# A three-stage transformer kernel on one core: both token tiles share the first weight units, a broadcast by TensorE, one sine, decay rows by way of memory, an alternating solve, other buffers

## The chip, the core and the metric

The kernel runs on one core of a Trainium2 chip. A core has five engines with a queue each: TensorE (PE; its weight loads are PEld), VectorE (DVE), ScalarE (ACT), GpSimd (POOL) and SyncE (SP, which here issues most DMAs). The metric is the device time of one execution in microseconds.

## The reference

All arrays are float32, with 256 tokens of width 1024. A first block runs two layers, each of four sublayers with a norm before and after: a gated FFN (1024 to 2816 and back), a mixer, a cross attention to 256 memory rows, and a second gated FFN. A second block (a state-space branch and a windowed attention, then an FFN) follows.

```python
h = swiglu(rms_norm(x, norm_pre[l, 0]), ffn1_gate[l], ffn1_up[l], ffn1_down[l])
x = x + 0.5 * rms_norm(h, norm_post[l, 0])
h = parallel_head_groups(rms_norm(x, norm_pre[l, 1]), ...)      # the mixer
...
# in the mixer, four heads in two directions (forward and flipped), chunks of 64 tokens:
g = jnp.cumsum(g)                                               # log decays
decay = jnp.exp(jnp.where(tril, g[..., :, None] - g[..., None, :], -jnp.inf))
lower = jnp.where(strict, (k_beta @ k.T) * decay, 0.0)
sol = lax.linalg.triangular_solve(lower, rhs, lower=True, unit_diagonal=True)
```

## The kernel before

Tokens lie in two tiles of 128 (t = 0, 1). A float32 product is made of three passes over a high and a low part of each operand (`mm3`, L170 to L172). Weights arrive in units of 512 KB: SP loads a unit into one of four `raw` buffers (L143), ACT writes its high part (L148), DVE its low part (L149), in two halves each. The split units live in a pool: `wp` has 4 units, `w2`, open during the FFNs and the cross attention, has 8. A unit's buffer is free when its last product has read it.

The instruction order on each engine is not the program's. The library simulates the program when it is built: each engine takes the first instruction, in program order, whose inputs and buffers are ready in that simulation. `issue_after(ins)` and `fence` only add an order behind an instruction of the same engine. On the chip each engine then runs its queue strictly in that order.

**FFN.** The 2816 channels are eleven groups j. For j = 0 and 1 `by_tokens(t, j)` makes the products with the tokens as stationary side, 24 matmuls of 512 columns over four weight units, then tanh on ACT (L364) and two DVE steps (L365, L366); a tail (`flush`) transposes the result (L371). For j = 2 to 10 `by_channels(i, j)` uses 48 matmuls of 256 columns. `DN(t, j)` is the down projection, 12 matmuls of 512 columns over two units. Program order: by_tokens(0,0), by_tokens(0,1), DN(0,0), by_tokens(1,0), by_tokens(1,1), DN(0,1); for each j the two `by_channels`, with DN(0, j-1) and DN(1, j-1) between up to j = 7, and DN(0,7) at j = 8; then DN(0,8), (0,9), (0,10), `fin(0)`, DN(1,7), (1,8), (1,9), (1,10). `fin(t)` adds the residual and starts the next stage's norm: squares on ACT (L205), a reciprocal root by small steps on POOL, x (L300) and its product with the next gain, xg (L235, or L237 where the root is put in at once), on DVE. `take_pre(t)` transposes xg on PE (L250). `fin(1)` of a stage is kept in `late` and runs in the next one (`run_late`).

**Start.** 16 warm-up matmuls on zeros; SP issues x of tile 0, the first gain as a broadcast to 128 partitions (512 KB, L221), two weight units, x of tile 1, two units.

**Hooks.** The first FFN of a layer runs `setup` between its groups: rotary tables (a sine per token tile, L675, with an ACT table load), the mixer's parameters, the memory's norm.

**Mixer.** `fill` is a stream of projections, whose products keep PE busy; hooks between its quarters run the rest. `strengths` makes the log decays g; `decays(d)` lays out, for each direction, three sets of rows (cumulated g of a token tile, four heads, 128 columns, the same in all partitions) in PSUM: four matmuls against a triangle each (L805), and for two of them a matmul that adds a mask (L807). ACT takes the exponential into `E`, and `pairs` (DVE, L997) multiplies it in. `solve` works on the two directions' 64-row halves: steps of a product with `M` (L1145) or with an inverse (L1153), four heads for each direction.

## Time and profile before

| what | before |
|---|---|
| median of 3 runs | 1947.57 us (1945.8 to 1948.2) |
| the profiled execution's own time | 1947.42 us |
| its span, first to last instruction | 1945.2 us |
| PE busy | 1914.7 us (98%) |
| DVE, ACT, POOL busy | 73%, 54%, 10% |
| TensorE clock granted, mean | 0.998 |
| HBM read | 333.90 MB, 172 GB/s over the span |

The profile is of one execution. Busy time of PE is a union of modelled durations, so the distance between the starts of neighbouring matmuls says more than the busy share. "Idle before" a group is what its engine waited, with the releaser that ended most of it.

### The profile page before, as it was taken

The page shows a single profiled execution, that of the slowest core. Times are in us where ns is not written, and L with a number is a line of the kernel's source. Part 1 is how long each engine was busy: PE and PEld are TensorE (multiplying, and loading weights), DVE is VectorE, ACT ScalarE, POOL GpSimd, SP SyncE. Part 2 cuts the span into 40 slices and gives each one's busy share as a digit, 9 for nine tenths or more (in the row PEclk, how much of TensorE's full clock was granted, in tenths as well). Part 3 has the DMA queues.
Part 4 walks back from the last instruction along what each step waited for, and adds up shares of the span by engine and source line. Part 5 has one row for each costly group of instructions (what it writes and reads, how often), then busy time and mean ns, then how long its engine had stood idle before and what let it go on. Part 6 is the DMA issues. An engine that isn't in the chain of part 4 may idle for free.

```text
span 1945.2 us, 34675 instructions
## 1 busy us (share of the span) xinstructions
PE 1914.7 (98%) x12859; PEld 1717.7 (88%) x12859; DVE 1412.7 (73%) x3002; ACT 1048.9 (54%) x2173; POOL 185.7 (10%) x407
## 2 busy tenths in 40 slices
PE   9999999999999999999999999999999999999998
PEld 6899888898899989999788978998999998888997
DVE  6777688775666766667987757666798988767765
ACT  5655465465554555546555645554555555546542
POOL 2000100020200110010100120002101111001000
PEclk9999999999999999999999999999999999999999
DMA  8666434364566556644434726655566646656651
GB/s 266 206 220 217 125 109 147 109 220 137 164 205 196 180 186 220 187 161 144 137 101 145 247 86 212 200 189 157 146 174 182 187 121 205 200 196 224 199 179 49
DMA packets 272887, 337.26 MB, mean 173 GB/s; under 512 B 19740, under 2 KB 223150, under 8 KB 272718
## 3 DMA queue, kind: packets, MB, share of 16 engines
q1 hardware_dynamic: 266980, 326.64, 53.6%
q10 hardware_dynamic: 5690, 8.25, 1.2%
q8 instruction: 101, 1.65, 0.3%
q14 instruction: 68, 0.56, 0.1%
q0 software_dynamic: 48, 0.16, 0.0%
HBM read 333.90 MB, written 1.08 MB: 172 GB/s over the span
## 4 chain that ended last, share of the span: by engine, by line
PE 84%; DVE 4%; POOL 3%; DMA 2%; ACT 2%; issue 2%; SPq 0%; ACTq 0%; POOLq 0%; DVEq 0%
PE bank L170 25%; PE bank L171 25%; PE bank L172 25%; DVE lo L149 2%; DMA raw<-in_ffn_up_dram 2%; PE bank L250 1%; POOL t L192 1%; POOL vh L213 1%; POOL y L193 1%; ACT hi L148 1%; PE bank L1003 1%; PE bank L1543 1%; ACT md L1034 1%; PE bank L1153 1%; PE bank L1256 1%
## 5 line engine op out<-in xcount | busy, mean ns | idle before, releaser
L148 ACT ACTIVATE hi<-raw 128x512 fp32r<-128x512 f32 (+1 forms) x1190 | 678.7, 615 | 413.6 <-PE bank L172 96.0
L149 DVE TENSOR_TENSOR lo<-raw,hi 128x512 fp32r<-128x512 f32 (+1 forms) x1190 | 764.7, 680 | 187.1 <-ACT hi L148 178.4
L170 PE MATMUL bank<-xh,hi 128*128 128x256 f32 x2080 | 588.8, 283 | 0.0
L171 PE MATMUL bank<-xl,hi 128*128 128x256 f32 x2080 | 585.1, 281 | 0.0
L172 PE MATMUL bank<-xh,lo 128*128 128x256 f32 x2080 | 584.7, 281 | 0.1
L170 PEld LDWEIGHTS bank<-xh,hi 128*128 128x128 f32 x2080 | 394.2, 190 | 4.1
L171 PEld LDWEIGHTS bank<-xl,hi 128*128 128x128 f32 x2080 | 393.9, 189 | 3.5
L172 PEld LDWEIGHTS bank<-xh,lo 128*128 128x128 f32 x2080 | 394.5, 190 | 0.6 <-DVE lo L149 0.6
L170 PE MATMUL bank<-hi,xh 128*128 128x512 f32 (+1 forms) x852 | 333.5, 392 | 3.5 <-ACT xh L175 2.2
L171 PE MATMUL bank<-lo,xh 128*128 128x512 f32 (+1 forms) x852 | 324.7, 381 | 5.2 <-DVE lo L149 5.1
L172 PE MATMUL bank<-hi,xl 128*128 128x512 f32 (+1 forms) x852 | 323.9, 380 | 0.5 <-DVE xl L177 0.5
L171 PEld LDWEIGHTS bank<-lo,xh 128*128 128x128 f32 x852 | 160.3, 188 | 34.8 <-DVE lo L149 9.9
L170 PEld LDWEIGHTS bank<-hi,xh 128*128 128x128 f32 x852 | 160.2, 188 | 31.5 <-ACT xh L175 3.5
L172 PEld LDWEIGHTS bank<-hi,xl 128*128 128x128 f32 x852 | 159.9, 188 | 28.8 <-DVE xl L177 2.2
L170 PE MATMUL bank<-hi,hh 128*128 128x512 f32 x440 | 175.9, 400 | 1.3 <-ACT hh L175 1.3
L171 PE MATMUL bank<-lo,hh 128*128 128x512 f32 x440 | 173.9, 395 | 0.0
L172 PE MATMUL bank<-hi,hl 128*128 128x512 f32 x440 | 173.4, 394 | 0.0
L213 POOL TENSOR_SCALAR vh<-ss 128x1 f32<-128x1 f32 x40 | 27.6, 689 | 1130.8 <-ACT junk L205 996.1
L402 ACT ACTIVATE th<-s 128x256 f32<-128x256 f32 x90 | 37.3, 414 | 124.3 <-DVE s L401 122.7
L172 PEld LDWEIGHTS bank<-hi,hl 128*128 128x128 f32 x440 | 82.7, 188 | 20.7 <-DVE hl L177 0.3
L170 PEld LDWEIGHTS bank<-hi,hh 128*128 128x128 f32 x440 | 82.7, 188 | 18.4 <-ACT hh L175 1.7
L171 PEld LDWEIGHTS bank<-lo,hh 128*128 128x128 f32 x440 | 82.7, 188 | 16.0
(369 smaller groups left out, 1991.4 us busy)
## 6 DMA issues: line engine op xcount, KB each, us to landing
raw<-in_w_in_dram SPq DMA_DIRECT2D x112, 512.0 KB, 4.4
raw<-in_ffn_gate_dram SPq DMA_DIRECT2D x176, 256.0 KB, 3.9
raw<-in_ffn_up_dram SPq DMA_DIRECT2D x176, 256.0 KB, 4.3
raw<-in_ffn_down_dram SPq DMA_DIRECT2D x88, 512.0 KB, 4.6
raw<-in_w_in_dram SPq DMA_DIRECT2D x96, 192.0 KB, 2.8
raw<-in_w_ffn_gate_dram SPq DMA_DIRECT2D x44, 256.0 KB, 3.8
raw<-in_w_ffn_up_dram SPq DMA_DIRECT2D x44, 256.0 KB, 4.1
raw<-in_w_ffn_down_dram SPq DMA_DIRECT2D x22, 512.0 KB, 4.6
```

What stands on the lines that cost most here:

```text
L148: nc.scalar.activation(hi[:, c], raw[:, c], AF.Copy)
L149: nc.vector.tensor_tensor(lo[:, c], raw[:, c], hi[:, c].bitcast(F32), ALU.subtract)
L170: mm(out, lhsT=lh, rhs=rh, start=start, stop=False)
L171: mm(out, lhsT=lh, rhs=rl, start=False, stop=False)
L172: mm(out, lhsT=ll, rhs=rh, start=False, stop=stop)
L192: V.tensor_scalar(t, y, y, vh, ALU.mult, ALU.mult)
L193: V.tensor_scalar(y, t, -1.5, y, ALU.add, ALU.mult)
L213: V.tensor_scalar(vh, s[:, 0:1], s[:, 1:2], 0.5 * EPS, ALU.add, ALU.add)
L250: self.nc.tensor.transpose(b[:, i * P:(i + 1) * P], src[:, (q + i) * P:(q + i + 1) * P], self.ident)
L402: last["A"] = nc.scalar.activation(th, s[:, 0], AF.Tanh)
L1003: T.matmul(b[:, j * 256:(j + 1) * 256], lhsT=lhs[:, h, j * P:(j + 1) * P], rhs=rhs[:, h], start=True, stop=True)
L1034: A.activation(md[r, :, :, :, s], mn[r, :, :, c0:c0 + 16].rearrange("p n h a -> p a h n"), AF.Copy, scale=self.half[s][r])
```

## The change

1. In a stage without a `late` part (only the first FFN of all), by_tokens of the two tiles run side by side, unit by unit (`by_tokens_parts`), before DN(0,0).
2. At the start the first gain comes as one row of 4 KB; two matmuls with a column of ones lay it out in two PSUM banks, between 12 warm-up matmuls instead of 16. SP issues the row, x of tile 0, one unit, x of tile 1, three units.
3. The rotary tables of both tiles are computed together, with one sine, which is moved behind a `yield` to the next hook.
4. The decay rows: four matmuls give the 16 rows for both directions and tiles, ACT copies them out, a DMA from POOL's queue writes them to memory, two more from the same queue read them back as broadcasts. POOL adds the masks (four additions of 128x512 in a layer). `strengths` hooks move: its third part one quarter earlier, `decays(0)` one quarter later.
5. In `solve` the matmuls of a step take turns between the directions, by `issue_after`.
6. In an FFN with a `late` part, the squares for the next norm are queued behind the tanh of by_tokens(0,0) (`behind`).
7. Buffers: gate and up units of j = 1 to 9 all go to `w2`, down units of j = 2 to 7 to `wp`; before, every third unit went to `wp`, and down units of j = 7 to `w2`. Gate and up of j = 10 stay in `wp`. The `raw` pool moves to the other end of SBUF.

The rotary part is cut below, and `solve`'s second loop, which has the same edit as its first.

```diff
-        self.rawp = pool(ctx, "raw", 4)
+        self.rawp = ctx.enter_context(tc.tile_pool(name="raw", bufs=4, side="right", reuse_waits="tile"))
+        self.behind = []
...
-        self.identr = self.fp.tile([P, P], F32R, name="identr")
-        self.mskr = [self.fp.tile([P, P], F32R, name=f"mskr{d}") for d in range(2)]
+        self.msk = [self.fp.tile([P, P], F32, name=f"msk{d}") for d in range(2)]
...
     def halves(self, a):
+        if isinstance(a, list):
+            return a
...
         if defer:
-            r = self.rstd(self.halves(self.x[t]), D, pool)
+            with ExitStack() as es:
+                for ins in self.behind:
+                    es.enter_context(self.tc.issue_after(ins))
+                r = self.rstd(self.halves(self.x[t]), D, pool)
...
             def wpool(kind, j):
-                cnt[0] += 1
-                if j == 1 or kind == "dn" and (j > 6 or j == 0):
-                    return w2
-                return self.wp if j == 10 or cnt[0] % 3 == 0 else w2
+                if kind == "dn":
+                    return self.wp if 1 < j < 8 else w2
+                return self.wp if j == 10 else w2
...
             def by_tokens(t, j, between={}):
+                for _ in by_tokens_parts(t, j, between):
+                    pass
+
+            def by_tokens_parts(t, j, between={}):
...
                     self.mm3(bb, xh[:, k, ix], xl[:, k, ix], wh[:, k % 2], wl[:, k % 2], k == 0, k == 7)
+                    if k % 2:
+                        yield
...
-            by_tokens(0, 0)
-            done = [last["A"].ins, last["V"].ins]
-            self.run_late()
-            by_tokens(0, 1, {4: flush, 6: lambda: self.take_pre(1)})
+            alone = self.late is None
+            if alone:
+                one, two = by_tokens_parts(0, 0), by_tokens_parts(1, 0)
+                next(one)
+                self.take_pre(1)
+                self.fence = self.last
+                for _ in range(3):
+                    next(two)
+                    next(one)
+                next(two)
+                for _ in range(2):
+                    next(one, None)
+                    next(two, None)
+                done = [last["A"].ins, last["V"].ins]
+                one, two = by_tokens_parts(0, 1), by_tokens_parts(1, 1)
+                for n in range(5):
+                    next(one, None)
+                    if n == 2:
+                        flush()
+                        flush()
+                    next(two, None)
+            else:
+                by_tokens(0, 0)
+                done = [last["A"].ins, last["V"].ins]
+                self.behind = done[:1]
+                self.run_late()
+                self.behind = []
+                by_tokens(0, 1, {4: flush, 6: lambda: self.take_pre(1)})
             self.fence = done
             DN(0, 0)
-            by_tokens(1, 0)
-            flush()
-            by_tokens(1, 1)
+            if not alone:
+                by_tokens(1, 0)
+                flush()
+                by_tokens(1, 1)
             flush()
...
-        for t in range(2):
-            wk = self.nrm.tile([P, 512], F32, tag="junk", name="wk")
...
-            nc.scalar.activation(cs, ang, AF.Sin)
-            self.cs1.append(cs)
+        ang, k = (wk[:, c:c + 256].rearrange("p (t c) -> p t c", t=2) for c in (0, 256))
...
+        yield
+        nc.scalar.activation(cs, ang, AF.Sin)
+        self.cs1 = [cs[:, t] for t in range(2)]
...
                 V.tensor_scalar(ngl, pg[:, 0:16].rearrange("p (t c) -> p t c", t=2), -1.0, None, ALU.mult)
+                b, r = self.bank(), w512()
+                for d in range(2):
+                    for t in range(2):
+                        T.matmul(b[0:4, (2 * d + t) * P:(2 * d + t + 1) * P], lhsT=g[:, t, d * 4:d * 4 + 4], rhs=self.tri[d], start=True, stop=True)
+                A.copy(r[0:4], b[0:4])
+                rows_d = dp.tile([2, 2, 4, P], F32, name="rows_d")
+                nc.gpsimd.dma_start(rows_d.rearrange("d t h c -> h (d t) c"), r[0:4].rearrange("h (x c) -> h x c", c=P))
+                for d in range(2):
+                    rows.append(ch4())
+                    nc.gpsimd.dma_start(rows[d], rows_d[d].rearrange("t h c -> (t h c)").unsqueeze(0).to_broadcast([P, D]))
                 yield
                 decays(0)
...
-                def rows(t, masked):
-                    b = self.bank()
-                    for h in range(4):
-                        T.matmul(b[:, h * P:(h + 1) * P], lhsT=g[:, t, d * 4 + h:d * 4 + h + 1].to_broadcast([P, P]), rhs=self.tri[d], start=h == 0, stop=h == 3 and not masked)
-                    if masked:
-                        T.matmul(hd(b), lhsT=self.identr, rhs=self.mskr[d].unsqueeze(1).to_broadcast([P, 4, P]), start=False, stop=True)
-                    return hd(b)
...
+                R = rows.pop(0).rearrange("p (t h c) -> p t h c", t=2, h=4)
+                mask = self.msk[d].unsqueeze(1).to_broadcast([P, 4, P])
+                V.tensor_tensor(ngc[:, c], R[:, f, :, end], ngl[:, f, c], ALU.add)
+                nc.gpsimd.tensor_tensor(R[:, f], R[:, f], mask, ALU.add)
                 for h in range(4):
...
+                nc.gpsimd.tensor_tensor(R[:, s], R[:, s], mask, ALU.add)
...
-                values(0, between=lambda: self.take_pre(1)), *qkv(1, {0: s}), *qkv(2, {0: s, 1: s, 3: s}),
+                values(0, between=lambda: self.take_pre(1)), *qkv(1, {0: s, 3: s}), *qkv(2, {2: s, 3: s}),
...
+                turns = [(h, d) for h in range(4) for d in range(2)]
+                in_turn = lambda one: self.tc.issue_after(one.ins) if one else nullcontext()
...
-                            for h in range(4):
-                                for d in range(2):
-                                    o = order[d][0]
-                                    T.matmul(bs[d][r[d], h * P:(h + 1) * P], lhsT=M[d][o, h, cols[d] + r[d].start:cols[d] + r[d].stop], rhs=y[d][o, h], start=True, stop=True)
+                            one = None
+                            for h, d in turns:
+                                o = order[d][0]
+                                with in_turn(one):
+                                    one = T.matmul(bs[d][r[d], h * P:(h + 1) * P], lhsT=M[d][o, h, cols[d] + r[d].start:cols[d] + r[d].stop], rhs=y[d][o, h], start=True, stop=True)
...
-        for _ in range(16):
-            nc.tensor.matmul(b, lhsT=zero[:, :P], rhs=zero, start=True, stop=True)
...
-    load_x(0)
-    g0 = net.bcast(net.gp, pre_of(stages[0]), D, "gain", nc.sync)
-    net.stash = [u() for u in units[:2]]
-    load_x(1)
-    net.stash += [u() for u in units[2:]]
...
+        nc.sync.dma_start(row, pre_of(stages[0]))
+        load_x(0)
+        early = [units[0]()]
+        load_x(1)
+        early += [u() for u in units[1:]]
+        net.stash = early
...
+        b, g0 = net.bank(), [net.bank() for _ in range(2)]
+        ins = None
+        for n in range(12):
+            with tc.issue_after(ins) if ins else nullcontext():
+                ins = nc.tensor.matmul(b, lhsT=zero[:, :P], rhs=zero, start=True, stop=True).ins
+            if n in (4, 5):
+                with tc.issue_after(ins):
+                    ins = nc.tensor.matmul(g0[n - 4], lhsT=one, rhs=row[:, (n - 4) * 512:(n - 3) * 512], start=True, stop=True).ins
```

## Rows read from the trace of the kernel before

**Rows 1.** The page's first part: busy time, share of the span, instructions.

```profile
PE 1914.7 (98%) x12859; PEld 1717.7 (88%) x12859; DVE 1412.7 (73%) x3002; ACT 1048.9 (54%) x2173; POOL 185.7 (10%) x407
```

**Rows 2.** Waits of PE, whole span: total us, times, longest us.

```profile
PE bank L171 <- DVE lo L149: 5.1, 7, 1.2
PE bank L371 <- DVE h L366: 4.7, 3, 1.7
PE bank L250 <- DVE xg L237: 2.7, 3, 1.3
...
PE bank L170 <- ACT hh L175: 1.3, 1, 1.3
```

**Rows 3.** Timeline of the start: start us, us, engine, operation [idle before, releaser].

```profile
6.48 1.29 DVE L235 TENSOR_TENSOR xg<-x,gain 128x512 f32<-128x512 f32 x2 [5.37 <-DMA gain<-in_norm_pre_dram]
...
8.71 1.15 ACT L148 ACTIVATE hi<-raw 128x512 fp32r<-128x512 f32 x2 [0.19 <-DMA raw<-in_ffn_up_dram]
...
9.39 0.50 PE L170 MATMUL bank<-hi,xh 128*128 128x512 f32 x1 [0.90 <-ACT hi L148]
```

**Rows 4.** Windows of the start: stretch, length, busy (count) per engine, clock, DMA share.

```profile
9.39:24.48 15.09, 14.00 (x58) 9.54 (x58) 14.04 (x24) 12.60 (x26) 8.83 (x13) 1.00 1.00 321
24.48:42.06 17.58, 17.56 (x77) 13.97 (x77) 12.76 (x27) 9.73 (x20) 0.00 (x0) 1.00 0.64 202
```

**Rows 5.** Timeline of ACT, the second sine.

```profile
83.58 1.28 ACT L675 ACT_TABLE_LOAD   x1
```

**Rows 6.** Timeline of PE, one of four decay blocks.

```profile
238.40 1.05 PE L805 MATMUL bank<-cst,g 128*128 128x128 f32 x8
239.21 0.47 PE L807 MATMUL bank<-mskr,identr 128*128 128x512 f32 x1
...
241.53 0.28 PE L170 MATMUL bank<-xh,hi 128*128 128x256 f32 x1
```

**Rows 7.** DMA issues: count, KB each, us from issue to landing.

```profile
rows<-rows_d SPq DMA_DIRECT2D x8, 512.0 KB, 4.9
...
cst<-in_consts_dram POOLq DMA_DIRECT2D x1, 152.0 KB, 5.6
...
rows_d<-w SPq DMA_DIRECT2D x1, 32.0 KB, 1.5
```

**Rows 8.** Timeline of POOL and DVE together, second block.

```profile
1421.21 1.05 POOL L1526 TENSOR_TENSOR w<-xs,dsk 128x512 f32<-128x512 f32 x1 [16.74 <-PE bank L1543]
1421.35 2.05 DVE L149 TENSOR_TENSOR lo<-raw,hi 128x512 fp32r<-128x512 f32 x2 [0.36 <-ACT hi L148]
```

**Rows 9.** Windows of the first layer's mixer, columns as in rows 4.

```profile
240.00:260.00 20.00, 20.00 (x140) 18.48 (x139) 15.69 (x39) 15.38 (x41) 0.00 (x0) 1.00 0.39 124
...
276.00:300.00 24.00, 21.90 (x101) 17.21 (x100) 23.31 (x84) 14.73 (x29) 2.84 (x4) 1.00 0.49 147
```

**Rows 10.** Timeline of PE in the solve: a mixed step and a separate one.

```profile
332.38 1.09 PE L1153 MATMUL bank<-ch,iv 64*64 64x128 f32 x16
333.40 0.50 PE L170 MATMUL bank<-hi,xh 128*128 128x512 f32 x1
...
338.69 1.08 PE L1145 MATMUL bank<-ch,M 64*64 64x128 f32 x8
339.70 0.50 PE L171 MATMUL bank<-lo,xh 128*128 128x512 f32 x1
```

**Rows 11.** Timeline of DVE at the third FFN's start.

```profile
686.62 1.28 DVE L235 TENSOR_TENSOR xg<-x,gain 128x512 f32<-128x512 f32 x2
688.01 0.42 DVE L365 SCALAR_TENSOR_TENSOR th<-th,bank 128x256 f32<-128x256 f32 x1
```

**Rows 12.** Timeline of ACT, DVE and PE at the fourth FFN's end.

```profile
1335.31 0.60 ACT L205 ACTIVATE junk<-bank 128x512 f32<-128x512 f32 x1 [0.77 <-PE bank L172]
...
1344.61 1.41 DVE L237 SCALAR_TENSOR_TENSOR xg<-x,y,gain 128x512 f32<-128x512 f32 x2 [4.05 <-POOL y L193]
...
1346.25 1.03 PE L250 MATMUL bank<-cst,xg 128*128 128x128 f32 x8
```

More of the change, by code (lines that the diff above doesn't have):

```diff
@@ L1 @@
 import math
-from contextlib import ExitStack
+from contextlib import ExitStack, nullcontext
 import numpy as np
@@ L323, in ffn @@
             pend = []
-            cnt = [0]
             last = {}
@@ L1150, in solve @@
                         bs = [self.bank() for _ in range(2)]
-                        for h in range(4):
-                            for d in range(2):
-                                T.matmul(bs[d][r[d], h * P:(h + 1) * P], lhsT=Z[d][r[d], h, n], rhs=rhs[d][r[d], h], start=True, stop=True)
+                        one = None
+                        for h, d in turns:
+                            with in_turn(one):
+                                one = T.matmul(bs[d][r[d], h * P:(h + 1) * P], lhsT=Z[d][r[d], h, n], rhs=rhs[d][r[d], h], start=True, stop=True)
                         A.copy(y[0][r[0]], hd(bs[0])[r[0]])
@@ L1765, in setup @@
         if l == 0:
-            net.rotary_tables()
+            yield from net.rotary_tables()
         yield from net.mixer_params(l)
```

65 lines of the change are left out of this document (31 added, 34 removed).

## The prediction, made before the changed kernel ran

> **What bounds the kernel now.** I read the page first. PE is busy for 98% of the span, DVE for 73% [rows 1]. Busy time of pipelined matmuls overlaps, so I then asked where PE's queue really waits, and where its matmuls start further apart than they need to. The waits of PE [rows 2] are few and short: no single kind sums to more than 5.1 us of 1945. So the kernel is bound by the number of matmuls in PE's queue nearly everywhere, and what takes matmuls out is worth their start-to-start time. It is worth less only where another engine is as full as PE. The windows show two such places. In the first 24 us the DMA engines are 100% busy and PE passes only 58 matmuls in 15.1 us, where the next stretch passes 77 in 17.6 [rows 4]. In the mixer DVE is busy for 23.3 of 24 us while PE waits 2.1 us [rows 9].
>
> All sums go against the profiled execution's own time, 1947.42 us (span 1945.2 and 2.2 around it). The median of the three runs, 1947.57, is 0.15 above it.
>
> **The start (1 and 2).** Xg of tile 0 waits 5.37 us for the gain broadcast, the first unit is ready at 8.71 - 0.19 = 8.52, and the first product starts at 9.39 [rows 3]. The broadcast is 512 KB; at the 321 GB/s of [rows 4] that is 1.6 us of a queue that is full. A 4 KB row in its place lets the unit land 1.6 us earlier, so the first product starts at about 7.8. Bounds: 0, if warm-ups and the two gain matmuls hold the transposes up, and 1.9, if the issue slot counts too. Then the feed: matmuls of 512 columns start 0.23 us apart (17.58/77 [rows 4]) and a transpose takes 0.1 (8 in 1.03 with the last one's tail [rows 12]). The 58 matmuls of the first stretch are 48 large and 10 small, or 12.1 us of work in 15.1; the second stretch loses about 0.4. Together 3.4 us wait for weights, one unit per 1.6 us for 1.4 us of work (six matmuls). With both tiles on a unit it is 2.8 us of work per unit, so the feed stops being short. What is late next is tile 1: its x lands behind unit 0, 1.6 us after it, then come xg (1.29 [rows 3]), a transpose group, and the split into parts, which puts it at about 11.7. PE has 12 matmuls of tile 0 until then, 2.7 of the 3.9 us, and loses 1.2. Gain 1.6 + 3.4 - 1.2 = 3.8 us; bounds 1.5 and 5.3.
>
> **One sine (3).** Each sine loads a table, 1.28 us of ACT [rows 5], and the one shown holds up the copy that PE waits 1.3 us for [rows 2]. The other one costs PE nothing. One of two goes, and the one left moves to another hook. Between 0 and 1.3, I take half: 0.6 us.
>
> **Decays (4).** One block of decay matmuls runs from 238.40 to 241.53, 3.13 us [rows 6]; four such blocks (two directions, two layers, all 3.13) are 12.5 us of PE. Added are four float32 matmuls in a layer, eight records; eight such records take 239.21 - 238.40 = 0.81 us [rows 6], 1.6 for both layers. PE gains 10.9 us. The way through memory: the second block of this kernel does the same with 1.5 us for the write and 4.9 for a broadcast of 512 KB [rows 7], some 7 to 8 us with the copy and the issues. The rows are asked for three quarters of a projection after they are made, each 24 matmuls of 256 columns or 2.9 us, so 8.7 us. It fits, barely; if it does not, ACT stands with the exponentials at its head, the splits of the next units behind them, and PE behind those once the units already split are used up. I cost it at nothing. The mask additions move to POOL, eight of them in all. An addition of this size on POOL, 1.05 us, stretched two DVE splits to 2.05 us [rows 8], where two operations of that size take 1.29 [rows 3], so it costs DVE up to 0.76, and nothing where DVE reads PSUM. At half, 1.5 us in a layer. DVE idles 4.3 us in 240 to 260 [rows 9], where PE becomes 5.4 us shorter, and it is full soon after. So I take back 0.8 us in a layer, 1.6 in all. Gain 9.3; bounds 3 (DVE sets the pace) and 10.9.
>
> [...]
>
> **The solve (5).** A step of which both directions' matmuls are mixed passes 16 records in 1.02 us (332.38 to 333.40). A step run one direction after the other takes 1.01 us for 8 (338.69 to 339.70) and the same again for the rest [rows 10]. Of the six steps in a layer three are mixed and three separate, in both layers. Six separate halves vanish: 6 x 1.01 = 6.1 us, and up to 0.2 each for the extra switch between shapes, 7.3. Waits for the later direction now stand at PE's head; other projections cover them where the build's simulation is right. I take 6.5; bounds 5 and 7.3.
>
> **Squares behind the tanh (6).** At three FFN starts PE waits for h, 4.7 us in all [rows 2]. The tanh comes after the squares, which wait for x. But DVE's queue is the same: xg ends at 687.90 and L365 starts at 688.01 [rows 11], so the tanh alone, earlier, gives 0.1 us each, unless the build also puts L365 before xg (up to 1.3 each). I take 0.3; bounds 0 and 3.9.
>
> **Buffers (7).** Down units of j = 7 now lie in `wp`. They are read last by DN(1,7), which stands after the last by_channels, and gate and up of j = 10 want all four units of `wp`. So two of those four units cannot be split until DN(1,7) has run. The build's simulation will find by_channels(0,10) half blocked and put DN(0,8), DN(0,9), DN(1,7) and probably DN(1,8) ahead of it. No matmul is added and PE stays busy there. What goes is the cover behind DN(0,10): four DN of 12 x 0.23 = 2.8 us each. At the fourth FFN's end the chain from the last squares to the end of xg takes 1346.02 - 1335.31 = 10.7 us, and PE takes up its transpose 0.2 us later [rows 12]: the four DN cover it exactly. With two left, 5.5 us lie open, of which 1.3 come back as the next tile's wait [rows 2]: 4.2. At the second FFN's end xg does not wait for POOL's root, 4.05 us less [rows 12]: 6.6 against 5.5, 1.1 us. The first and third FFN are followed by the mixer's value projection, which does not need x, and the last one ends the kernel with fin(1): nothing. Cost 5.3; bounds 0 (DN(1,7) finds a free place earlier) and 9. The new place of `raw` I cost at nothing: no row shows an operation that depends on an address.
>
> **Sum.** 1947.42 - 3.8 - 0.6 - 9.3 - 6.5 - 0.3 + 5.3 = 1932.2 us.
>
> **The rivals.**
> A, the sum, 1932.2, own range 1928 to 1936.
> B, the cover at the FFN ends is not lost, because DN(1,7) and (1,8) stay or something else covers the chain: 1926.9. For it: before, PE took the last down projections in program order, and nothing in the trace shows how the build reorders them; against it: the buffer count above.
> C, DVE takes the mixer's gain: decays give 3 and the sum is 1938.5, and to 1943.5 if the FFN ends cost more as well. For it: 23.3 of 24 us [rows 9]; against it: DVE still idles in 240 to 260. [...]
> D, the rows come late. If each hop takes the 5.6 us of the one load issued by POOL [rows 7], the way is 12 us against 8.7 and ACT stands for 3.5 us in each layer: 1939. Against it: units already split feed PE meanwhile. [...]
> E, slower: with gate and up of j = 2 to 9 in `w2` alone, PE waits for a split unit in every group. There are five FFNs with eight such groups, 40. From 15.2 + 3.9 = 19.1 us, or 0.48 us a group, the kernel is slower by over 0.2%; at 0.6 it takes 1956. Against it: two groups fit in `w2`, and a unit is freed a whole group (two by_channels and two DN, 17 us) before its successor is read, while its split takes 1.3.
>
> **How the numbers follow.** A 0.42, B 0.28, C 0.18 (0.04 of it above 1943.5), D 0.07 (0.01 above), E 0.05. The bound of 0.2%, 3.9 us, is about what a measurement of this kernel can tell from no change. Faster is 0.42 + 0.28 + 0.14 + 0.06 = 0.90, same 0.05, slower 0.05. The likeliest case gives 1932. The range goes from 1924 (B with the start and the solve at their upper bounds) to 1940 (C and D inside it); about 0.08 lies below and 0.11 above.
>
> **What would show it.** Right: first product near 7.8 us and by_channels beginning near 38 in place of 42; L805 and L807 gone and 16 records in their place; all solve steps as one group of 16; DN(1,7) before the end of by_channels(1,10) in PE's order, and a wait of L250 for xg of 4 to 6 us at the start of the second block. Wrong: DVE full from 235 to 300 with PE waits beyond 2 us in each mixer (C); ACT idle on the rows' landing for more than 2 us (D); PE waits for `lo` spread over the FFN groups (E); no wait at the second block (B).

## The result: slower by 0.9%, and the profile after

The changed kernel takes 1964.97 us (median of 4 runs, 1963.70 to 1967.29), the kernel before 1947.88 beside it: ratio 1.0089, 95% interval 1.0077 to 1.0101. The forecast was 1932, and its range ended at 1940. The profiled execution took 1965.46 us, with a span of 1963.3 and a mean granted clock of 0.994 (before 0.998).

The page's first part, after:

```profile
PE 1918.8 (98%) x12771; PEld 1715.1 (87%) x12771; DVE 1420.9 (72%) x2992; ACT 1049.2 (53%) x2171; POOL 199.5 (10%) x421
```

PE has 88 matmuls less than in [rows 1] and is busy for 4.1 us more: busy time hides where the loss is. PE's waits over the span of the kernel after (total us, times, longest us):

```profile
PE bank L172 <- DVE lo L150: 8.0, 8, 2.0
PE bank L171 <- DVE M L1040: 6.7, 2, 3.4
PE bank L381 <- DVE h L376: 4.9, 4, 1.5
PE bank L173 <- DVE lo L150: 4.2, 3, 3.0
PE bank L253 <- DVE xg L240: 3.6, 3, 2.3
```

Against [rows 2], waits of 3.0 and 3.4 us are new, and there are more of the others. All kinds together they sum to 36.2 us, against 22.1 before. These 14.1 us more do not explain the loss by themselves: the shift counted below is 18.1 us, although PE has some 14 us less to do (10.6 in the decays, 3.9 in the solve).

What does is a comparison of starts. Both traces hold 10392 records of the three-pass matmuls (L171 to L173 after, L170 to L172 before). I paired the n-th with the n-th and noted how much later it starts. The table gives, for each stretch, the us by which this shift grows against the kernel before. The first column goes to the 150th matmul, the others to that time of the kernel before; the last is the sum, at the last matmul. The kernels e1 to e12 are the experiments below, and each row is one profiled execution.

```
stretch     start  to 134   to 230     to 400  to 520 to 706    to 890     to 1056 to 1177 to 1307 to 1386   rest  sum
                   sine     1st FFN    mixer,  cross  2nd FFN   3rd FFN    mixer,  cross   4th FFN 2nd block
                            end        layer 0 att.             and end    layer 1 att.            start
after       +2.2   -2.8     +6.4       +1.1    +0.5   +1.0      +4.2       +0.8    +0.9    -0.1    +3.2     +0.7 +18.1
e1 pools    +2.4   -2.7     +1.0       +2.5    +0.8   -0.4      -0.1       +2.1    -0.7    -0.2    +2.1     +0.2  +7.0
e2 matmul   +1.9   -3.3     +3.9       -1.9    +1.9   -0.2      +2.2       -2.2    +0.5    -0.9    +3.1     -0.7  +4.3
e3 quarter  +1.6   -2.8     +7.0       +4.4    -0.3   +1.1      +2.8       +4.5    +2.2    -0.1    +3.7     +0.6 +24.7
e4 DVE      +2.1   -2.8     +5.8       -1.4    +0.2   +0.8      +2.8       -1.4    -0.5    -0.1    +5.0     +0.7 +11.3
e5 start    -0.2   -2.8     +6.2       +1.6    +0.9   +0.9      +3.1       +1.2    +0.8    -0.1    +3.2     +0.6 +15.5
e6 hooks    +1.8   -0.9     +2.8       +1.0    +0.6   +1.2      +2.7       +0.8    -0.5    -0.1    +1.4     +0.7 +11.5
e7 kept     -0.0   -1.0     +0.9       -1.4    +1.7   -0.2      +0.0       -2.2    +2.2    +0.0    -0.0     -0.3  -0.3
e8 at hand  +1.9   -2.8     +7.2       -0.7    +0.5   +1.2      +5.4       -1.7    +2.3    -0.1    +3.2     +0.6 +17.0
e9 warm-ups +0.5   -2.6     +7.4       +1.2    +2.3   +0.9      +3.2       +0.9    +0.3    -0.1    +3.6     +0.6 +18.2
e10 feed    -0.2   -2.5     +0.9       -1.9    +0.5   -0.1      +0.0       -2.2    -0.8    +0.0    +0.0     -0.3  -6.7
e11 both    +1.6   -2.8     +7.3       -2.3    -0.1   +0.8      +3.6       -3.9    +0.9    -0.1    +3.5     +0.7  +9.2
e12 kept    -0.3   -2.5     +0.9       -1.9    +0.2   -0.2      -0.0       -2.2    +0.6    +0.0    -0.0     -0.3  -5.9
```

The gain of the removed matmuls is nowhere to be seen, and three places lose: the start, the mixers, and the ends of the FFNs.

**The clock.** Some waits here cost more than their length. Windows of the kernel after around the first FFN's end (stretch, length, busy and count of PE, PEld, DVE, ACT, POOL, granted clock, DMA share, GB/s):

```profile
170.00:178.00 8.00, 8.00 (x70) 8.00 (x68) 5.17 (x10) 4.49 (x12) 0.14 (x1) 1.00 0.59 195
178.00:183.00 5.00, 1.74 (x13) 1.33 (x11) 2.37 (x5) 1.24 (x4) 2.32 (x8) 1.00 0.31 105
183.00:186.00 3.00, 2.88 (x19) 2.88 (x20) 1.88 (x4) 1.03 (x2) 0.00 (x0) 0.77 0.68 201
186.00:190.00 4.00, 4.00 (x27) 4.00 (x27) 1.38 (x3) 1.35 (x3) 0.00 (x0) 0.75 0.66 242
```

PE stands for 3.3 us from 179.82, and behind it the mean clock is 0.77 and 0.75: PE passes 27 matmuls in 4 us where it passes 70 in 8 at a clock of 1.00. Start to start the matmuls lie 0.21 us apart from 184.7 to 187.9, against 0.12. From 30 us on, the kernel before has nine distances of more than 1.5 us between starts, none above 2.26, and in the 8 us behind each of them the clock is 1.00. Behind the longest, which ends at 1113.52:

```profile
1113.60:1117.60 4.00, 4.00 (x34) 3.94 (x35) 3.29 (x7) 3.77 (x8) 0.00 (x0) 1.00 0.69 209
```

**The FFN's end.** Timeline of the kernel after (start us, us, engine, operation, [idle before, releaser]):

```profile
178.65 0.39 PE L171 MATMUL bank<-xh,hi 128*128 128x256 f32 x1 [0.37 <-ACT hi L149]
...
181.05 1.41 DVE L240 SCALAR_TENSOR_TENSOR xg<-m,y,gain 128x512 f32<-128x512 f32 x2 [2.52 <-POOL y L194]
182.38 1.29 DVE L150 TENSOR_TENSOR lo<-raw,hi 128x512 fp32r<-128x512 f32 x2
...
183.12 0.39 PE L173 MATMUL bank<-xh,lo 128*128 128x256 f32 x1 [3.02 <-DVE lo L150]
```

PE waits for the last two units of j = 10 (`hi` at 178.65, `lo` at 183.12), and `lo` stands in DVE's queue behind the memory's xg, which waits 2.52 us for POOL. The 178.65 wait comes behind 186 matmuls of this run of by_channels, which has 240 (five times 48). If by_channels(0,10) ran through first, its third unit would be wanted behind 144 + 24 = 168; 192 is the first half of both by_channels of j = 10. So the build put nearly all of both first halves ahead of the third unit. By the code, the reason is the buffers: `wp` has four, the units of j = 7 hold two of them until DN(1,7), and so the last two units of j = 10 wait for the buffers of the first two.

**The start.** Timeline of the kernel after:

```profile
3.42 2.07 PE L1854 MATMUL bank<-row,one 1*128 1x512 f32 x2
...
5.53 0.69 DVE L238 TENSOR_TENSOR xg<-x,bank 128x512 f32<-128x512 f32 x1 [4.28 <-PE bank L1854]
5.96 2.07 PE L1854 MATMUL bank<-row,one 1*128 1x512 f32 x2
...
7.96 2.74 PE L1851 MATMUL bank<-zero 128*128 128x512 bf16 x6
...
10.50 1.91 PE L253 MATMUL bank<-cst,xg 128*128 128x128 f32 x8
...
12.24 0.79 PE L171 MATMUL bank<-hi,xh 128*128 128x512 f32 x1
...
13.26 1.37 PE L253 MATMUL bank<-cst,xg 128*128 128x128 f32 x8
```

A gain matmul is two float32 records of 1.0 us each. The four take the place of the broadcast as what xg waits for, xg is done at 8.76 (8.07 and 0.69), and its transposes stand behind six warm-ups until 10.50. The first product starts at 12.24 in place of 9.39 [rows 3].

PE's matmuls lie about twice as far apart in all of this as later. The warm-ups lie 0.42 us apart from start to start up to 10.50, and the transposes 0.21 up to 13.7 and 0.11 from 14.0 on; in the kernel before the warm-ups lie 0.43 apart at first and 0.22 from 4.06 on, and its first eight transposes take 1.26 us. (The trace's first clock record, of 1.00, begins at 13.9 us, and in the kernel before at 4.0; for the time ahead of it the windows print 1.00.) In all nine profiles with the new start the closer spacing begins between 11.5 and 13.9 us, in the five with the old one between 4.0 and 6.7. It is not six warm-ups too many (in e9 the transposes lie 0.21 us apart as well); which part of the new start holds the closer spacing back is not tested.

**The mixer.** Timelines of the kernel after, PE, ACT, POOL and DVE one behind the other:

```profile
238.42 1.04 PE L807 MATMUL bank<-cst,g 128*4 128x128 f32 x8
...
249.76 0.56 ACT L808 COPY w<-bank 4x512 f32<-4x512 f32 x1
...
250.63 0.64 POOL L810 DMA_DIRECT2D rows_d<-w  x1 [30.59 <-ACT w L808]
254.72 1.08 POOL L813 DMA_DIRECT2D ch<-rows_d  x2 [3.45 <-DMA rows_d<-w]
260.68 3.56 POOL L853 TENSOR_TENSOR ch<-ch,msk 128x512 f32<-128x512 f32 x2 [4.88 <-DVE ssk L871]
...
263.02 1.33 DVE L1028 TENSOR_TENSOR cc<-be,rk 128x8 f32<-128x8 f32 x2
264.28 1.26 DVE L190 TENSOR_SCALAR y<-sh 128x8 int32<-128x8 int32 x1
...
268.37 0.40 PE L173 MATMUL bank<-hi,xl 128*128 128x512 f32 x1
272.12 0.50 PE L171 MATMUL bank<-hi,xh 128*128 128x512 f32 x1 [3.36 <-DVE M L1040]
```

The rows are made at 238.4 as in [rows 6], but their copy stands in ACT's queue until 249.76, the write takes 3.45 us, and the broadcasts are issued at 254.72. DVE and ACT arrive at the rows' first readers before they land (waits from 255 to 275; total, times, longest):

```profile
DVE ngc L852 <- DMA ch<-rows_d: 3.9, 2, 3.6
```
```profile
ACT E L855 <- DVE ngc L852: 2.3, 1, 2.3
```

Then POOL's additions take 1.26 to 1.75 us each, beside them two DVE operations that take 0.23 us in e4 take 1.33 and one of 0.16 takes 1.26, and the pairs come so late that PE stands from 268.37 to 272.12, with half clock behind (window 274 to 276):

```profile
274.00:276.00 2.00, 2.00 (x9) 1.45 (x8) 2.00 (x7) 2.00 (x5) 0.00 (x0) 0.50 0.00 0
```

### The profile page after: what moved, and what is told of

It is laid out like the page before. It is cut to its first block, busy times and chain, and to the rows that moved or that the text cites. A ratio compares the mean times of both kernels' runs of the same rounds, so it can differ in the third digit from the quotient of the medians.

```text
span 1963.3 us, 34511 instructions
## 1 busy us (share of the span) xinstructions
PE 1918.8 (98%) x12771; PEld 1715.1 (87%) x12771; DVE 1420.9 (72%) x2992; ACT 1049.2 (53%) x2171; POOL 199.5 (10%) x421
## 4 chain that ended last, share of the span: by engine, by line
PE 77%; DVE 7%; issue 5%; DMA 4%; POOL 4%; ACT 3%; SPq 0%; ACTq 0%; POOLq 0%; DVEq 0%
PE bank L171 23%; PE bank L173 23%; PE bank L172 23%; DVE lo L150 3%; PE bank L253 1%; POOL t L193 1%; POOL vh L214 1%; ACT hi L149 1%; DMA raw<-in_xattn_o_dram 1%; DMA raw<-in_ffn_up_dram 1%; POOL y L194 1%; DMA raw<-in_ffn_down_dram 1%; ACT md L1076 1%; PE bank L1589 1%; DMA ch<-rows_d 1%
## 5 line engine op out<-in xcount | busy, mean ns | idle before, releaser
L171 PE MATMUL bank<-xh,hi 128*128 128x256 f32 x2080 | 590.9, 284 | 2.3 <-ACT hi L149 2.3
L173 PE MATMUL bank<-xh,lo 128*128 128x256 f32 x2080 | 586.1, 282 | 4.3 <-DVE lo L150 4.2
L172 PE MATMUL bank<-xl,hi 128*128 128x256 f32 x2080 | 586.2, 282 | 0.0
L171 PEld LDWEIGHTS bank<-xh,hi 128*128 128x128 f32 x2080 | 395.3, 190 | 7.6 <-ACT hi L149 3.1
L173 PEld LDWEIGHTS bank<-xh,lo 128*128 128x128 f32 x2080 | 395.3, 190 | 5.6 <-DVE lo L150 5.1
L172 PEld LDWEIGHTS bank<-xl,hi 128*128 128x128 f32 x2080 | 395.3, 190 | 3.2
L171 PE MATMUL bank<-hi,xh 128*128 128x512 f32 (+1 forms) x852 | 335.0, 395 | 9.7 <-DVE M L1040 6.7
L172 PE MATMUL bank<-lo,xh 128*128 128x512 f32 (+1 forms) x852 | 326.8, 384 | 8.0 <-DVE lo L150 8.0
L173 PE MATMUL bank<-hi,xl 128*128 128x512 f32 (+1 forms) x852 | 325.5, 383 | 0.5 <-DVE xl L178 0.5
L171 PEld LDWEIGHTS bank<-hi,xh 128*128 128x128 f32 x852 | 161.4, 190 | 37.9 <-DVE M L1040 7.6
L172 PEld LDWEIGHTS bank<-lo,xh 128*128 128x128 f32 x852 | 161.7, 190 | 36.9 <-DVE lo L150 12.0
L173 PEld LDWEIGHTS bank<-hi,xl 128*128 128x128 f32 x852 | 161.2, 189 | 29.1 <-DVE xl L178 2.3
L173 PE MATMUL bank<-hi,hl 128*128 128x512 f32 x440 | 173.8, 395 | 0.7 <-DVE hl L178 0.7
L171 PE MATMUL bank<-hi,hh 128*128 128x512 f32 x440 | 173.9, 395 | 0.0
L172 PE MATMUL bank<-lo,hh 128*128 128x512 f32 x440 | 173.4, 394 | 0.0
L411 DVE TENSOR_TENSOR s<-bank,rows 128x512 f32<-128x512 f32 x90 | 61.8, 686 | 85.0 <-PE bank L173 51.2
L173 PEld LDWEIGHTS bank<-hi,hl 128*128 128x128 f32 x440 | 82.7, 188 | 19.8 <-DVE hl L178 1.2
L171 PEld LDWEIGHTS bank<-hi,hh 128*128 128x128 f32 x440 | 82.7, 188 | 16.4 <-ACT hh L176 0.2
```

Source lines behind the costliest of these rows:

```text
L171: mm(out, lhsT=lh, rhs=rh, start=start, stop=False)
L172: mm(out, lhsT=lh, rhs=rl, start=False, stop=False)
L173: mm(out, lhsT=ll, rhs=rh, start=False, stop=stop)
L411: nc.vector.tensor_tensor(s, bb, rows[0], ALU.mult)
```

## The experiments

Theories, named in the expectations: P, the pools lose the FFN ends; H, the yield in the rotary tables, by which every later hook of the first FFN runs one group later, loses the first one; R, the rows come late; L, POOL's additions slow DVE; C, ACT and DVE set the pace once the decay matmuls are gone; S, the alternation's waits. All ratios are to the kernel before, run on the same chip; the changed kernel's is 1.0089.

**e1, old pools.**

```diff
-                if kind == "dn":
-                    return self.wp if 1 < j < 8 else w2
-                return self.wp if j == 10 else w2
+                cnt[0] += 1
+                if j == 1 or kind == "dn" and (j > 6 or j == 0):
+                    return w2
+                return self.wp if j == 10 or cnt[0] % 3 == 0 else w2
```

> The changed kernel with the old assignment of weight units to `wp` and `w2`. Theory P (the pools): in all four FFN ends of the first block PE waits because the last two units of j = 10 have no buffer, and each wait costs again in clock. By the shift of matched matmuls between the two traces that is 5.5 (first FFN's end) + 1.0 + 4.3 + 1.0 and 1.7 at the start of the second block, 13.5 us: expected 1951 to 1954, no PE gap over 1 us in the last five by_channels of any FFN. Rival H (the hooks, moved one place later by the new yield in the rotary tables, make the first FFN's loss): the gap of 3.3 us near 180 stays, and with the clock behind it 5.5 us of the 13.5 stay: 1957.

Measured: 1951.85 us, 1.0029 (1.0016 to 1.0042), 11.7 us less (0.60% of 1947.5). In the table the FFN ends fall from +6.4, +4.2 to +1.0, -0.1, with the hooks where the change put them. PE has no wait over the whole stretch from 150 to 215. P holds, H alone does not. The second block's start keeps 2.1 of 3.2, which P does not explain. The mixers lose 1.4 and 1.3 us more: in the first stand gaps of 3.78 and 3.02 us, with low clock behind both. Windows of e1:

```profile
268.00:272.00 4.00, 4.00 (x13) 3.04 (x12) 3.40 (x11) 3.18 (x6) 0.00 (x0) 0.50 0.01 2
...
284.00:288.00 4.00, 4.00 (x12) 2.73 (x12) 4.00 (x15) 3.57 (x8) 0.00 (x0) 0.64 0.43 131
```

**e2, matmul decays.**

```diff
-                R = rows.pop(0).rearrange("p (t h c) -> p t h c", t=2, h=4)
...
+                b = rows(f, True)
...
-*qkv(1, {0: s, 3: s}), *qkv(2, {2: s, 3: s})
+*qkv(1, {0: s}), *qkv(2, {0: s, 1: s, 3: s})
```

> The changed kernel with the decay rows laid out by matmuls as before (hooks as before; the position tables' two small columns moved to another tile for room). Theory R (rows late): the way by memory saves 10.6 us of PE and costs 15.5 in the mixers (7.9 and 7.6), so undoing it gives about 5 us: expected 1959 to 1962, and the PE gaps of 3.75 and 3.73 us in the mixers gone. Rival S (the alternation's waits at PE's head make the mixer's loss): the gaps stay, and 10.6 us of matmuls come back: 1973 to 1976.

Measured: 1951.32 us, 1.0030 (1.0021 to 1.0040). The time is below R's range. The mixers go from +1.1 and +0.8 to -1.9 and -2.2, 6.0 us in all, about the 5 that R has, and their gaps of 3.7 us are gone, so S falls. The other 5.5 us of the ratio lie outside what was edited, mostly at FFN ends (+6.4 and +4.2 become +3.9 and +2.2), where a wait of nearly the same length does or does not bring the clock down: the gap of 3.20 us at 178.3 is still there, and behind it the clock is 1.00. PE's waits from 235 to 320 in e2:

```profile
PE bank L174 <- DVE lo L152: 2.1, 2, 1.2
```

**e3, rows a quarter earlier.**

```diff
-*qkv(1, {0: s, 3: s}), *qkv(2, {2: s, 3: s})
+*qkv(1, {0: s, 2: s}), *qkv(2, {2: s, 3: s})
```

> The changed kernel with the rows made one quarter of a projection earlier (the hook of the third part of strengths from quarter 3 to 2); in ACT's order the copy of the rows then stands behind the first tanh of the convolutions instead of the second, some 9 us earlier. Theory R (rows late): they land near 252 instead of 260.4, the gaps of 3.7 us and the half clock behind them go, and most of 7.9 + 7.6 us is given back: 1951 to 1956. Rival L (the four mask additions on POOL slow DVE): they are still there and beside the same DVE work, so at least half of the loss stays: 1958 to 1965.

Measured: 1971.08 us, 1.0125 (1.0110 to 1.0140), slower than the changed kernel by 7, and outside both ranges. The rows land at 251.8, as meant, and the mixers lose 3.3 and 3.7 us more. R as I had put it falls: an earlier row does not help, because the build moved its readers forward too. PE's, DVE's and ACT's waits from 235 to 285:

```profile
PE bank L171 <- ACT hi L149: 5.5, 1, 5.5
```
```profile
DVE ngc L852 <- DMA ch<-rows_d: 3.7, 1, 3.7
```
```profile
ACT E L855 <- DVE ngc L852: 3.1, 1, 3.1
```

DVE waits 3.7 us for the rows as before (3.6), ACT 3.1, and now the 24 exponentials stand ahead of a weight split that PE needs: one gap of 5.9 us, with a clock of 0.50 in the 8 us behind it.

**e4, masks on DVE.**

```diff
-                nc.gpsimd.tensor_tensor(R[:, f], R[:, f], mask, ALU.add)
+                V.tensor_tensor(R[:, f], R[:, f], mask, ALU.add)
```

(and the same for `s`)

> The changed kernel with the four mask additions of a layer on DVE instead of POOL. Rival L (POOL's additions slow DVE): operations of 0.16 us that took 0.7 to 1.3 beside them take 0.16 again, the pairs come earlier, 5 us or more come back: 1955 to 1960. Theory R (rows late): the rows land at 260.4 as before and the gap of 3.7 us stays within 1 us of that; DVE has 4 x 0.7 us more of its own and loses some 4 us of stretch in a layer: 1962 to 1967.

Measured: 1958.19 us, 1.0057 (1.0040 to 1.0073), 6.2 us less, inside L's range. Timeline of DVE in e4:

```profile
259.82 0.16 DVE L852 TENSOR_TENSOR ngc<-ch,ngl 128x4 f32<-128x4 f32 x1 [3.62 <-DMA ch<-rows_d]
...
263.04 0.23 DVE L1028 TENSOR_TENSOR cc<-be,rk 128x8 f32<-128x8 f32 x2
263.19 0.16 DVE L190 TENSOR_SCALAR y<-sh 128x8 int32<-128x8 int32 x1
```

The wait for the rows is the same 3.62 us, the stretched operations take 0.16 again, the gap of 3.75 us is 0.91, and the mixers stand at -1.4 each, 4.7 us less in both. DVE's busy time over the span hardly changes (1418.7 us against 1420.9), but in e4 it holds the eight additions, 0.69 us each or 5.5 us: beside POOL's additions DVE's own operations took some 7.7 us longer in both layers. PE goes on at 268.61 in place of 272.12, and its waits from 235 to 320 fall from 7.8 to 3.9 us. The clock is not what is won: it falls in e4 too, behind shorter waits, and stays low for longer. Window of e4:

```profile
276.00:285.00 9.00, 7.17 (x22) 5.23 (x21) 6.70 (x15) 7.92 (x18) 0.85 (x2) 0.62 0.23 60
```

**e5, old start** (loads, gain, warm-ups, and by_tokens of tile 0 first).

> The changed kernel with the old start: 16 warm-ups, the gain as a broadcast, x and units in the old order, by_tokens of tile 0 before tile 1. Theory T (the four records of the two gain matmuls, 1.0 us each, and the six warm-ups queued behind them hold the first transposes until 10.50): the new start loses 2.2 us to matched matmuls by 48, so the time falls by about 2 us against the changed kernel, which would be 1.008 of the kernel before. Rival (the start gains as forecast and the loss is elsewhere): it rises by 2 to 4 us.

Measured: 1962.34 us, 1.0076 (1.0061 to 1.0091); the interval reaches to that of the changed kernel. In the table the start is -0.2 in place of +2.2. That the new start loses 2.2 us is shown in the trace; the time says only that it does not gain 2 to 4.

**e6, hooks back.**

```diff
-            yield from net.rotary_tables()
+            net.rotary_tables()
...
-        yield
         nc.scalar.activation(cs, ang, AF.Sin)
```

> The changed kernel without the yield ahead of the sine, so that every later hook of the first FFN runs one group earlier, as before. Rival H (the moved hooks make the first FFN's loss of 5.5 us): the gap of 3.3 us at 180 goes and the half clock behind it; the sine's wait of 1.7 us at 84 comes back: 3.5 to 4 us faster than the changed kernel. Theory P alone (the pools): the two late units of j = 10 still cost, about as at the third FFN's end (4.3 us): 0 to 1 us faster from this place and 1.7 slower from the sine.

Measured: 1965.36 us, 1.0086 (1.0068 to 1.0104): no difference. Its profiled run is by far its fastest, 1958.92 at a clock of 0.997; the others took 1965.0 to 1967.2 at 0.991 to 0.994. In that run the gap of 3.3 us is gone and the first FFN's end loses 2.8 instead of 6.4, while the sine gives 0.9 instead of 2.8; the clock falls behind two waits, not six. Whether the hooks matter to the median is not settled.

**e7 and e12, the kept parts:** e1, e2 and e5 together, so that the sine, the alternation, the squares behind the tanh and the side of `raw` are left of the change.

> The changed kernel with the old pools, the old start and the matmul decays together; what is left of the change is the one sine behind its yield, the alternation in the solve, the squares behind the tanh, and the side of `raw`. If the losses are those of these three parts, what remains is the sine's 2.0 us and the solve's 3.9 (18.3 less 14.4 us of its matmuls): 1947.6 - 5.9 = 1941.7, 0.997 of the kernel before, 1940 to 1944. Rival (the alternation's waits at PE's head, or the side of `raw`, cost as well): 1945 or more.

> The kernel of the kept parts once more, for its interval and for a profile nearer its median (the first profile was its slowest run). 1941.8 again, 0.9975 of the kernel before. If the alternation is worth its 3.9 us of matmuls, the matched matmuls of the mixers' solve are 1.5 to 2 us earlier in each layer, and stay so behind the cross attention; in the first profile the cross attention gave 1.8 us of each back.

Measured: 1941.84 us, 0.9975 (0.9966 to 0.9984), and again 1941.89, 0.9975 (0.9965 to 0.9985). Faster than before by 0.25% both times, 4.9 us, as the parts had it (1941.7). The trace of the second shows from where: -2.5 in the sine's stretch, -1.9 and -2.2 in the mixers. The FFNs hold within 0.9, and the cross attention gives back 0.2 and 0.6. The first profile was of the slowest run, 1946.63: its shift ends at -0.3, with -1.0 at the sine and +1.7 and +2.2 in the cross attention. The side of `raw` costs nothing that shows beside these.

**e8, rows at hand.**

```diff
             def strengths():
+                for d in range(2):
+                    rows.append(ch4())
+                    nc.gpsimd.dma_start(rows[d], a["mem_norm"][l:l + 1].to_broadcast([P, D]))
```

> The changed kernel with the decay rows read from an input that is in memory from the start, by the same two broadcasts from POOL's queue, issued in the first part of strengths; copy and write remain, the numbers in the rows are not the decays, the exponentials take another scale and the masks another sign, so the output is not the reference's. Theory R (ACT and DVE stand with the rows' readers at their heads until the rows land, with the weight splits behind them): the waits of 3.6 (DVE) and 2.3 us (ACT) and the gaps of 3.7 us in both mixers go, and with the half clock at least 4 us in each mixer come back: 1952 to 1957. Rival L (POOL's additions are the cost): they run as before, and little more than nothing comes back: 1961 to 1966.

The rows read back are not the decays, so this kernel leaves the right result out and serves for its time alone. Measured: 1961.77 us, 1.0069 (1.0052 to 1.0086), 3.9 less; the interval overlaps that of the changed kernel, and the time lies in L's range and outside R's. The waits for rows and the gaps of 3.7 us are gone, and the mixers go to -0.7 and -1.7, 4.3 us in all where R wanted 8. Another gap, of 3.0 and 3.2 us, has grown some 16 us further on, with a clock of 0.81 and 0.79 in the 8 us behind it.

**e9, six warm-ups** (`range(6)` for `range(12)`).

> The changed kernel with 6 warm-ups in place of 12, so that none stands behind the two gain matmuls. Theory T (the start is late by the gain matmuls and by the warm-ups queued behind them): xg of tile 0 is ready at 8.76, the transposes begin there and not at 10.50, 1.7 us earlier, and the whole start with them: 1963 (1.0078 of the kernel before). Rival (the feed is late anyway: the DMA engines stand at 12% from 14 to 16 us, since SP waits for a free raw buffer): nothing comes of it, 1965.

Measured: 1965.54 us, 1.0092 (1.0078 to 1.0105). The transposes start early, and the shift at the 150th matmul is +0.5 and not +2.2. PE's timeline in e9:

```profile
7.96 1.97 PE L253 MATMUL bank<-cst,xg 128*128 128x128 f32 x8
```

These transposes, too, lie 0.21 us apart. The first FFN's end loses 7.4 (6.4), the cross attention 2.3 (0.5), where the clock is 0.79 in the 8 us behind a wait of 1.77 us. The 1.7 us were won and are not in the time.

**e10, the kept parts with both tiles side by side** (`alone = self.late is None`).

> The kernel of the kept parts with one thing more of the change: by_tokens of both tiles side by side in the first FFN, with the old loads, the old gain and the old warm-ups. The forecast's term for the feed: 3.4 us of waits for weights go and 1.2 are lost to tile 1, so 2.2 us faster than the kept parts: 1939.6, 0.9963 of the kernel before. Rival (no feed is won, because the splits of the later units stand in ACT's queue behind the split of the transposed tile): within 1 us of the kept parts, 0.997 to 0.998.

Measured: 1940.34 us, 0.9966 (0.9954 to 0.9978). By the table's reckoning the start is -0.2 and the sum -6.7. It beats the kernel before and the changed one; it is not told apart from the kept parts alone. The trace shows that the feed is won and lost again: at the 58th matmul the shift is -2.33 us (e12 -0.24), at the 150th -0.22 (e12 -0.26). PE has caught up with the splits. The last h is split in ACT's queue behind weight parts that wait 0.76 us for their load, and the down projection that reads it waits:

```profile
39.45 0.50 PE L173 MATMUL bank<-hi,hh 128*128 128x512 f32 x1 [1.60 <-ACT hh L178]
```

**e11, rows at hand and masks on DVE** (e8 and e4 together).

> The rows read from an input that is in memory from the start, and the masks on DVE (the rows are not the decays, as in the run with rows at hand). If late rows and POOL's additions are all that costs the mixers (theories R and L together), PE sets the pace again, and 7.9 + 7.6 us come back: 1949 to 1951. Theory C (once the decay matmuls are gone, ACT and DVE set the pace of the mixers, and what PE does not do there it waits): of the 10.6 us of removed matmuls at least half is still given back in waits: 1954 to 1958, with a gap of 2 us or more ahead of a weight part while ACT makes the 16 pieces of md.

Measured: 1956.38 us, 1.0045 (1.0030 to 1.0061), in the range of C. With rows on time and no POOL the mixers come to -2.3 and -3.9, so of 5.3 us of decay matmuls and 2 of the solve in a layer, 14.6 in both, 6.2 are in the time, less than half. A gap of 3.1 us remains in both layers; behind the first's the clock is 0.79 over 8 us, behind the second's 1.00, which is about what parts the two. Timeline of ACT in e11:

```profile
272.91 1.15 ACT L149 ACTIVATE hi<-raw 128x512 fp32r<-128x512 f32 x2 [5.20 <-DMA raw<-in_w_in_dram]
273.96 7.56 ACT L1076 ACTIVATE md<-M,cst 32x128 f32<-32x128 f32 x16
...
282.64 1.67 ACT L149 ACTIVATE hi<-raw 128x512 fp32r<-128x512 f32 x3
```

ACT waits 5.2 us for a load, makes the 16 pieces of md, and only then splits the unit that PE stands for from 280.4 to 283.6. The window behind it:

```profile
284.00:288.00 4.00, 4.00 (x12) 3.10 (x11) 4.00 (x19) 2.04 (x5) 0.00 (x0) 0.58 0.45 136
```

So C is right that others set the pace here. ACT is far from full from 260 to 280 (11.1 of 20 us), but it is busy for 7.88 of the 8 us from 276 to 284, and DVE for 18.4 of the 20 from 260. That it is the order of ACT's queue, with the 16 pieces ahead of the split, is read from the trace and not tested. The kernel before stands at this place too, with 1.63 us between starts from 279.69. That its decay matmuls, earlier in the mixer, were part of the cover is only argued.

## Why the prediction was wrong

**Start, -3.8 forecast, +2.2 measured.** The broadcast's end was seen rightly as what xg waits for; what failed is "the first product starts at about 7.8": it starts at 12.24. The lower bound named the gain matmuls and priced nothing: a float32 matmul of 512 columns was in no row, the nearest rows were the float32r ones at 0.23 us, and it takes 2.0 here, at the wide spacing that the new start keeps to 13.9. The feed came true as far as the shared units reach, 3.4 - 1.2 = 2.2 forecast: from the first product to the 58th matmul the shift falls from +2.85 to +0.05, in e10 from +0.04 to -2.33. What had no term is the step behind it: up to the 150th the shift is back at +2.21 (e10 -0.22), because the down projections, which by_tokens of tile 1 no longer covers, wait for h and its split (0.46 and 0.72 us, in e10 1.60).

**Sine, -0.6, measured -2.8.** Right in sign, too small in size. Without the yield (e6) it is -0.9. With it, it is -2.5 to -3.3 in all profiles but e7's, where the wait of 1.2 us is still there and the gain is 1.0.

**Decays, -9.3.** This is the step that failed: "It fits, barely". PE's 10.6 us went as counted (12.5 by L805 and L807, 1.9 by the new L807, start to start), and all of it came back, with the solve's gain. I counted the way from the matmuls; on the chip the copy stood 10.3 us in ACT's queue (239.46 to 249.76), the write took 3.5 and not 1.5, the broadcasts 6.1 and not 4.9. And I costed a late row by ACT's wait alone (D, 3.5 us per layer). That the weight splits behind ACT's exponentials would hold PE up was written down and then costed at nothing. What was missing is that DVE waits for the rows too (3.6 us), that the order of the queues moves with the build, so that earlier rows do not help (e3), that POOL's additions stand in the same chain (e4, 6.2 us of the time and 4.7 in the mixers), and that slow matmuls follow a gap of 3.7 us. Theories D and C were both named, at 0.07 and 0.18, with 7 and 6.3 us. D happens, by its own sign (2.3 us of ACT). C does not, by its sign: DVE is not full, with 55.6 of the 65 us from 235 to 300, before 56.3. The mixers stand at +1.9 with the new decays and at -4.1 without them (e2), so the decays cost 6.0 us where 9.3 were to be gained: 15.3 us, a little more than the two prices together.

The stretch of DVE beside POOL's additions was priced too low: half of 0.76 us for each of the eight is 3 us, of which 1.6 went into the sum, and by e4 it is some 7.7. Two TENSOR_TENSOR of 128x8 take 1.33 us beside an addition and 0.23 in e4. The forecast's "nothing where DVE reads PSUM" agrees with one place of the kernel before: operations of 128x256 that read a bank (L629 to L632) take 0.42 us each beside POOL's from 266.07 on, as they do from 264.74 without one. Two of 128x40 that read none (L1050) take 0.77 each beside POOL's from 294.16 on, where two of 128x120 take 0.28 and 0.27 at 279.63 without one.

**Solve, -6.5.** Mis-sized: 18.3 us of its matmuls became 14.4, 3.9 less, and e2 and e12 show 1.9 and 2.2 us in a layer. Timeline of PE in the solve of the kernel after:

```profile
341.18 1.09 PE L1199 MATMUL bank<-ch,iv 64*64 64x128 f32 x16
...
347.49 0.43 PE L1190 MATMUL bank<-ch,M 64*64 64x128 f32 x2
...
350.57 1.08 PE L1190 MATMUL bank<-ch,M 64*64 64x128 f32 x14
```

Three of the six steps in a layer run as one group of 16. The three others run as 2 and 14 (a float32 matmul is two records here, as in the x8 of L807 for four): the second matmul belongs to the direction that is late, and PE does other matmuls meanwhile. So such a step saves about 0.65 us against the separate halves of [rows 10], and not the 1.01 that I took: 3.9 us over six steps.

**Squares behind the tanh, -0.3.** Right: PE's waits for h are 4.9 us over four times against 4.7 over three; one of the four, 0.5, is the new one at the start, which leaves 4.4 over the same three, and in e12 they are 4.0.

**Pools, +5.3, measured about 12.** The premise held (two units of j = 7 keep half of `wp`), the order did not: I expected DN(1,7) to be taken forward and the cover behind DN(0,10) to go. The build kept the seven DN in a row and ran both by_channels of j = 10 in halves, so the loss lies inside them: it hits the first and third FFN, which I had costed at nothing, and the second block's start, named for 4.2 us, lost 3.2. In e1 11.7 us come back. How much of the first FFN's loss needs the moved hooks as well stays open (e6).

**The rivals.** E, the one on the slower side, had PE wait in every FFN group. It does not; its sign was right by luck, by another mechanism. C's upper value, 1943.5, does not follow from its terms: 1938.5 with the FFN ends at their bound of 9 is 1942.2.

**The clock.** No term had it: every price of a wait was its length. Before, the clock falls behind no wait until the kernel's end. After, it does at six places in the profiled execution (behind the gaps at 180, 268, 853, 941, 1137 and 1373). In the 8 us behind each the mean granted clock is 0.79, which is an estimated 0.21 x 8 = 1.7 us if PE has work throughout, some 10 in all, about half of the 18.1 of the table. That this much of the time is the clock's is not shown apart.

That the length of the wait decides is not shown: behind 1.77 us at 1137.21 the clock falls (0.72 and 0.78 from 1139 to 1146), behind 2.42 us at 284.69 it is 1.00.

## What to carry to other kernels

Where PE is at 98%, matmuls taken out of its queue are worth their time only if the producers behind them can run ahead: in e11, with the rows on time, less than half of it came. Look at the distance between the starts of paired matmuls in both traces, since busy shares hide both gain and loss. A step moved to another engine is priced by what stands behind its readers in their queues, not by the length of its own way. A wait of PE beyond those that the kernel before shows at full clock is priced by its length alone at one end of the range and with slow matmuls behind it at the other (here about 1.7 us each time).

## What the runs showed of the chip

The length of a gap did not decide by itself what the clock did behind it. In the kernel after, the gaps of 3.30, 3.75 and 3.73 us between matmul starts all have low clock behind them (0.79 over 8 us), and so have one of 2.67 us, two of 1.53 and 1.25 us close together (853 to 857), and one of 1.77 us at 1137.21 in the cross attention. One of 2.42 us has none, nor has the same gap of 1.77 us at the same place in layer 0 (463.86). Between kernels it differs too: behind e2's gap of 3.20 us the clock is 1.00, where behind the 3.30 of the kernel after it is 0.79 over 8 us. In e11 the gap of 3.14 us in layer 0 has low clock behind it, the 3.09 in layer 1 has not. What decides is left open. Windows of the kernel after:

```profile
287.00:289.00 2.00, 1.89 (x8) 1.42 (x8) 1.75 (x7) 1.98 (x5) 0.00 (x0) 1.00 0.39 76
...
857.00:860.00 3.00, 3.00 (x17) 3.00 (x16) 0.31 (x2) 0.90 (x2) 0.00 (x0) 0.51 0.77 274
...
1139.00:1142.00 3.00, 2.77 (x8) 1.92 (x9) 1.88 (x6) 1.43 (x5) 0.00 (x0) 0.72 0.35 118
...
1375.00:1378.00 3.00, 2.72 (x13) 2.39 (x14) 1.86 (x4) 1.27 (x3) 0.00 (x0) 0.64 0.20 71
```

A kernel with such waits also scatters: e6 took 1958.9 to 1967.2 us at mean clocks of 0.997 to 0.991, e1 1950.4 to 1956.2 at 0.998 to 0.993, and the order by clock is nearly the order by time. A part's worth of 1 to 2 us cannot be read from the time of such a kernel (e5, e9), only from its trace.
